# VectorE's order in the early stage of a hybrid diffusion step: activations ahead of partial sums, scan parameters later

## The chip, the cores and the metric

The kernel runs on one core of one Trainium2 chip. The metric is the time of one execution on the device in microseconds; the median of the runs is compared. The host's layout of the weights into tiles is done before and is not timed.

## What is computed

One layer of a hybrid trunk for 128 context tokens and 128 latent tokens with the same weights. The parts that matter here are those at the start:

```python
mod = silu(cond) @ w_mod + b_mod                 # (2048) @ (2048, 12288), for two conditions
sh1, sc1, g1, sh2, sc2, g2 = split(mod, 6)
xm = rmsnorm(x, norm_mix_g) * (1.0 + sc1) + sh1  # 2 x 128 tokens, 2048 channels
u, q, k, v, g_s, g_a = split(xm @ w_in)          # w_in: 2048 x 6656
```

After that come a bidirectional complex diagonal scan over `u` (64 groups of 64 states, with parameters `exp(lambda * dt)`, `B`, `C`), windowed attention over `q`, `k`, `v` with cached keys, gates, an output projection and a convolutional feed-forward block. The scan's parameters depend on the weights alone, not on the tokens.

## The kernel before, in words

**Precision.** Every large product is made of three products of fp32r halves: a weight tile `raw` is split into `hi` (ScalarE, line 184) and `lo` (VectorE, line 185), the activations into `xh`/`xl` (lines 391, 392), and TensorE adds `lo*xh`, `hi*xl`, `hi*xh` (lines 395 to 397 with weights stationary, 421 to 423 with activations stationary).

**Staging.** Columns of `xm` can be made as soon as their scale and shift columns are known. So the start of the kernel runs in seven phases over the 2048 input channels, in blocks of 128: `PHASES = (1, 1, 1, 1, 4, 4, 4)`. I count them from 0. In each phase eight groups of 512 output columns (k and v, two of q, two of u, three gates; `part_group`, line 478 on) get the products of this phase's blocks only. The result of the first phase is copied to an SBUF tile `pg`; in each later phase VectorE adds the accumulator banks to it (line 507, twice per group), and the last addition of u goes to a tile `u` (line 505). The accumulator banks are three of tag `acc` and one of tag `y`. The last phase's remaining units are taken into a later stage, woven with attention.

**Mod columns.** While a phase runs, the scale and shift columns of later phases are computed from `w_mod` (`mod_first` for one block, `mod_steps` for four; line 263): four narrow products at a time, 32 columns of the array each. Behind the last of them `mod_pp` (line 266) transposes the accumulated rows on VectorE (`macc`, line 268), adds them over the four strips with small products on TensorE (line 272) and adds the bias on VectorE into `modp` (line 276). The next phase begins with `make_xm` (line 377): scale `gsc` (line 379), the normalized transposed input `nT` scaled and shifted in place (line 390, one instruction per block and token set), the copy `xh` on ScalarE, the remainder `xl` on VectorE.

**Scan parameters.** `load_params`, `load_bc("B")`, `load_bc("C")` and `fine` of `SSM` are generators. Together they come to 22 pieces: 1 the loads of lambda, dt and states (POOL's queue); 2 to 8 some 130 small VectorE instructions on tiles `wk`, `keep`, `LB`, `LC`, `M` (128x64); 9 the loads of B (SP's queue, tile `bcn`, line 1231); 10 to 13 four blocks of copies (`cg`, ScalarE, line 1056), transpositions and copies (`bct`); 14 to 19 the same for C; 20 to 22 tables `FC` with a scratch tile `fw` (lines 1206 to 1219). `piece()` runs the next one. From phase `PIECE0` on one piece is placed behind every second unit of a phase; a phase of one block has 8 units (4 pieces), one of four blocks 16 (8 pieces). What is left is run at once behind the sixth unit of the last phase:

```python
            if p >= PIECE0 and i % PIECEN == 1:
                step(piece)
...
    step(lambda: [None for _ in gen])
```

**Order.** The program lists steps; the framework's scheduler orders each engine's queue at compile time by a simulated timeline, taking of the instructions that are ready the one with the highest priority, which is the earlier one in the program unless a block raises it. `tc.high_priority(n)` raises it by n places: splitting of weights has `HP = 300`, attention `ATTH = 300`, some later blocks `HP2 = 1000`. `tc.issue_after(ins)` keeps the instructions of the block that are on the same engine as `ins` behind it in that queue. Once ordered, each engine and each DMA queue works strictly in that order and waits where it must. Weight loads go through SP's queue in the order of the units that use them: a ring of 5 raw tiles, and 5 slots for mod weights. Tiles of 4 KB per partition (`nT`, `pg`, `nat`, `wk`, `M`, `bcn`, `bct`, `fw`, attention's `kT` and others) share a pool of 18 slots.

**Attention** starts with `att_setup` (cached keys loaded by POOL into `kT`, lines 594 and 595) and `att_k` (transposition and copy, line 604).

Of the kernel before, what the change touches and what calls it, by code (L numbers as in the profile page):

```python
# [14 lines left out]
OP = mybir.AluOpType  # L15
# [63 lines left out]
def burst(lst, pos):  # L79
    end = pos + 1  # L80
    while lst[end - 1].src is not None and lst[end - 1].frees == 0:
        end += 1
    return end


RAW, HL, W4, NS4, W2, LOADS = 5, 3, 18, 5, 3, 5
PHASES, NGA, MLEAD, PIECE0, PIECEN = (1, 1, 1, 1, 4, 4, 4), 3, 4, 2, 2
HP = 300
MRATE, AHEAD = 1.5, True
NGA2, NGS, SF0, ATT1 = 3, 4, 0.6, 1.0  # L90
# [2 lines left out]
G2A, G2B, G2S, G2C, LAG2, HP2 = 8, 8, 3, 2, 2, 1000  # L93
# [4 lines left out]
def tile_hybrid_step(ctx, tc, a):  # L98
    nc = tc.nc
    TT, TS, STT, CP = nc.vector.tensor_tensor, nc.vector.tensor_scalar, nc.vector.scalar_tensor_tensor, nc.vector.tensor_copy  # L100
# [8 lines left out]
    w4 = ctx.enter_context(tc.tile_pool(name="w4", bufs=W4))  # L109
# [12 lines left out]
    def T2(shape, name):  # L122
        return w2.tile(shape, F32, tag="w2", name=name)

    def XM(name):
        return xmp.tile([128, 4, NT], F32R, tag="xm", name=name)

    def PS(shape, tag, bufs=1):
        return ps.tile(shape, F32, tag=tag, name=tag, bufs=bufs)

    def f32(x):
        return x.bitcast(F32)
# [3 lines left out]
    def step(fn):  # L136
        steps.append(Step(fn))
# [60 lines left out]
    def wsrc(w, k0, c0, nk=2):  # L198
        v, j = w[k0 // 2, c0 // 512], k0 % 2
        return lambda raw: [(raw[:, 0:nk], v[:, j:j + nk, :])]  # L200
# [60 lines left out]
    def mod_mm(acc, kt, rhs, b, start, stop):  # L261
        j = kt % 4
        return MM(acc[32 * j:32 * j + 32], cst[:, kt, 6 - 2 * b:38 - 2 * b], rhs, start=start, stop=stop, skip_group_check=True,  # L263
           tile_position=(0, 32 * j))

    def mod_pp(acc, nb, blocks):
        m = T2([128, 512], "macc")[:, 0:acc.shape[1]]
        nc.vector.transpose(out=m, in_=acc)
        p = acc[:, 0:acc.shape[1] // 64 * nb].rearrange("p (c b s) -> p c b s", b=nb, s=2)
        mv = m.rearrange("p (c b r) -> p b c r", b=4, r=32)  # L270
        for b in range(4):
            MM(p[32 * b:32 * b + 32], i32r, mv[:, b, :, 0:2 * nb], start=True, stop=True, skip_group_check=True, tile_position=(0, 32 * b))
        for b0, c0, nc_, b, n in blocks:
            ks = slice(b0, b0 + nc_ * n)
            v = lambda t: t[:, ks].rearrange("p (b c) -> p c b", b=n)
            TT(modp[:, ks, :].rearrange("p (b c) s -> p c b s", b=n), p[:, c0:c0 + nc_, b:b + n, :],
               v(bT).unsqueeze(3).to_broadcast([128, nc_, n, 2]), OP.add)
# [18 lines left out]
    def mod_steps(gs, pool="raw"):  # L296
        nb = len(gs)
        st = {}

        def chunk(b, ku):  # L300
            def f(raw):
                if ku % 2 == 0:
                    st["r"] = raw
                    return
                if b == 0 and ku == 1:
                    st["a"] = PS([128, 512], "mod")
                prev = None
                for i, r in ((ku, raw), (ku - 1, st["r"])):
                    for j in range(2):
                        with tc.issue_after(prev.ins) if prev is not None else nullcontext():  # L310
                            prev = mod_mm(st["a"], 2 * i + j, r[:, j, :], b, b == 0 and i < 2, b + 1 == nb and i > 5)
                if b + 1 == nb and ku == 7:
                    one = all(g == gs[0] + i for i, g in enumerate(gs))
                    mod_pp(st["a"], nb, [(4 * gs[0], 0, 4, 0, nb)] if one else [(4 * g, 0, 4, i, 1) for i, g in enumerate(gs)])
            return f
        return [Step(chunk(b, ku), wsrc(a["w_mod"], 2 * ku, 512 * MOD_AT[g]), False, pool, frees=2 * (ku % 2)) for b, g in enumerate(gs) for ku in range(8)]

    def mod_first(k0, n):
        v = a["w_mod_first"]
        st = {}  # L320
        nk = 8 // n
        view = lambda raw: raw.rearrange("p a c -> p (a c)").rearrange("p (k c) -> p k c", k=nk)

        def chunk(part, ku):
            def f(raw):
                if part == 0 and ku == 0:
                    st["a"] = PS([128, 2, 128 * n], "mod")
                r = view(raw)
                for j in range(nk):
                    mod_mm(st["a"][:, part, :], nk * ku + j, r[:, j, :], 0, ku == 0 and part == 0 and j < 4, nk * ku + j >= 12)  # L330
                if part == 1 and ku == 2 * n - 1:
                    mod_pp(st["a"].rearrange("p a c -> p (a c)"), 1, [(16 + k0, 0, n, 0, 1), (k0, n, n, 0, 1)])
            return f

        def src(part, ku):
            return lambda raw: [(view(raw), v[part, k0, ku])]
        return [Step(chunk(p, ku), src(p, ku), False, "w4") for p in range(2) for ku in range(2 * n)]

    small = cpool.tile([128, 16], F32, name="small")
    nT = []  # L340
# [31 lines left out]
        nT.append(t)  # L372

    XH, XL = [], []
    gsc = cpool.tile([128, 16, 2], F32, name="gsc")

    def make_xm(k0, n):
        ks = slice(k0, k0 + n)
        STT(gsc[:, ks, :], modp[:, 16 + k0:16 + k0 + n, :], 1.0, gmix[:, ks].unsqueeze(2).to_broadcast([128, n, 2]),
            op0=OP.add, op1=OP.mult)  # L380
        m = min(n, 2)
        for k in range(k0, k0 + n, m):
            g4, o = k // 4, k % 4
            if o == 0:
                XH.append(XM("xh"))
                XL.append(XM("xl"))
            for c in range(m):
                for s in range(2):
                    v = nT[g4][:, o + c, 128 * s:128 * s + 128]
                    TS(v, v, gsc[:, k + c, s:s + 1], modp[:, k + c, s:s + 1], op0=OP.mult, op1=OP.add)  # L390
            ACT(XH[g4][:, o:o + m], nT[g4][:, o:o + m], AF.Copy)
            TT(XL[g4][:, o:o + m], nT[g4][:, o:o + m], f32(XH[g4][:, o:o + m]), OP.subtract)

    def mm3(o, wh, wl, xh, xl, start, stop):
        MM(o, wl, xh, start=start, stop=False, skip_group_check=True)  # L395
# [120 lines left out]
    def pieces(*gens):  # L516
        for g in gens:
            for _ in g:
                yield

    gen = pieces(ssm.load_params(), ssm.load_bc("B"), ssm.load_bc("C"), ssm.fine())

    def piece():
        next(gen, None)

    def sig(t):
        ACT(t, t, AF.Sigmoid)
# [27 lines left out]
    done, nw = 0, 0  # L555
    for p, n in enumerate(PHASES):
        k0 = sum(PHASES[:p])
        step(lambda k0=k0, n=n: make_xm(k0, n))
        w = [u for g in groups for u in g(k0, n)]
        if p + 1 == len(PHASES):  # L560
            steps.extend(w[:3 * n // 2])
            late = w[3 * n // 2:]
            break
        for i, x in enumerate(w):
            steps.append(x)
            nw += 1
            if xs and i % 2 == 0:
                step(xs.pop(0))
            if p >= PIECE0 and i % PIECEN == 1:
                step(piece)  # L570
            target = max(round(need[p] * (i + 1) / (len(w) - MLEAD)), round(MRATE * nw))
            while done < min(target, len(mq)) and (done < need[p] or i + 1 >= len(w) - MLEAD or AHEAD):
                end = burst(mq, done)
                steps.extend(mq[done:end])
                done = end
# [928 lines left out]
```

## Time and profile before

| | us |
|---|---|
| median of 3 runs | 1549.94 |
| lowest, highest | 1549.81, 1554.12 |
| the profiled execution's own time | 1552.15 |
| its span, first to last instruction | 1550.1 |
| mean granted TensorE clock (1 is full) | 0.99 |

All windows and starts below are microseconds from the start of this span. Engines: PE is TensorE's products, PEld its weight loads, DVE VectorE, ACT ScalarE, POOL GpSimd, SPq and POOLq the DMA queues of SyncE and GpSimd. A busy PE is a modelled figure, since products are pipelined; the starts are measured.

### The profile page before, as it was taken

The numbers are of one execution on the slowest core, as the hardware profiler recorded it, in microseconds if no ns is written. First come the engines' busy times: TensorE is split into PE (matmuls) and PEld (weight loads), VectorE is DVE, ScalarE is ACT, GpSimd is POOL, SyncE is SP. The second block draws the span as 40 slices with busy tenths as digits, with TensorE's granted clock in tenths as the row PEclk, the third lists the DMA queues.
The fourth block names the chain that finished last, engine by engine and source line by source line (L and its number), as shares of the span: only waits on it lengthen the run. The fifth ranks groups of instructions, "written<-read, shape, count | busy, mean of one in ns | idle before, by whom it ended". The sixth has DMA issues, their size and how long they took to land.

```text
span 1550.1 us, 29294 instructions
## 1 busy us (share of the span) xinstructions
PE 1491.0 (96%) x11871; PEld 1311.1 (85%) x11871; DVE 1007.7 (65%) x1541; ACT 766.7 (49%) x1191; POOL 85.7 (6%) x179
## 2 busy tenths in 40 slices
PE   6989999999899999999999999999999999999997
PEld 5758799778677788998689999889999988999986
DVE  4997776468866566765665656655665655666665
ACT  6335537645545666544554544433544543545543
POOL 2000004022321000000000000000000000000000
PEclk9999999999999999999999999999999999999999
DMA  9999754774676677975566676765555565566563
GB/s 352 352 340 321 286 196 157 258 277 156 209 241 238 240 250 274 310 244 192 172 242 235 205 245 201 238 200 190 176 192 181 181 197 191 175 205 197 170 203 123
DMA packets 104246, 349.18 MB, mean 225 GB/s; under 512 B 13900, under 2 KB 16628, under 8 KB 104112
## 3 DMA queue, kind: packets, MB, share of 16 engines
q1 hardware_dynamic: 98576, 344.20, 64.9%
q0 software_dynamic: 5312, 3.05, 0.8%
q8 instruction: 93, 1.52, 0.4%
q14 instruction: 41, 0.34, 0.1%
q10 hardware_dynamic: 224, 0.08, 0.0%
HBM read 343.76 MB, written 2.46 MB: 223 GB/s over the span
## 4 chain that ended last, share of the span: by engine, by line
PE 83%; DMA 8%; DVE 4%; ACT 2%; issue 1%; POOL 1%; SPq 0%; DVEq 0%; ACTq 0%
PE acc L395 16%; PE acc L396 16%; PE acc L397 16%; PE acc L421 8%; PE acc L422 8%; PE acc L423 8%; PE mod L263 5%; DMA raw<-in_w_mod_dram 2%; DMA raw<-in_w_in_dram 2%; PE bu L1375 1%; DVE lo L185 1%; DMA rw<-in_w_mod_dram 1%; DMA U<-u 1%; DMA raw<-in_w_attn_o_dram 1%; ACT hi L184 1%
## 5 line engine op out<-in xcount | busy, mean ns | idle before, releaser
L185 DVE TENSOR_TENSOR lo<-raw,hi 128x1024 fp32r<-128x1024 f32 (+1 forms) x456 | 538.7, 1186 | 444.8 <-ACT hi L184 442.8
L184 ACT ACTIVATE hi<-raw 128x1024 fp32r<-128x1024 f32 (+1 forms) x456 | 468.5, 1029 | 609.1 <-PE acc L397 260.7
L395 PE MATMUL acc<-yh,lo 128*128 128x256 f32 x1408 | 400.0, 284 | 0.0
L396 PE MATMUL acc<-yl,hi 128*128 128x256 f32 x1408 | 398.8, 283 | 0.0
L397 PE MATMUL acc<-yh,hi 128*128 128x256 f32 x1408 | 398.7, 283 | 0.0
L395 PEld LDWEIGHTS acc<-yh,lo 128*128 128x128 f32 x1408 | 270.3, 192 | 8.9 <-DVE lo L185 4.2
L396 PEld LDWEIGHTS acc<-yl,hi 128*128 128x128 f32 x1408 | 270.3, 192 | 0.1
L397 PEld LDWEIGHTS acc<-yh,hi 128*128 128x128 f32 x1408 | 270.2, 192 | 0.0
L395 PE MATMUL acc<-xh,lo 128*128 128x256 f32 x568 | 166.8, 294 | 9.3 <-ACT sig L672 4.8
L396 PE MATMUL acc<-xl,hi 128*128 128x256 f32 x568 | 163.4, 288 | 0.0
L397 PE MATMUL acc<-xh,hi 128*128 128x256 f32 x568 | 163.1, 287 | 0.0
L422 PE MATMUL acc<-lo,ff 128*128 128x512 f32 x352 | 136.8, 389 | 0.0
L423 PE MATMUL acc<-hi,ff 128*128 128x512 f32 x352 | 136.8, 389 | 0.0
L395 PEld LDWEIGHTS acc<-xh,lo 128*128 128x128 f32 x568 | 109.2, 192 | 31.4 <-DVE lo L185 6.9
L421 PE MATMUL acc<-hi,ff 128*128 128x512 f32 x352 | 127.8, 390 | 0.0
L396 PEld LDWEIGHTS acc<-xl,hi 128*128 128x128 f32 x568 | 109.6, 193 | 2.4 <-issue 2.2
L397 PEld LDWEIGHTS acc<-xh,hi 128*128 128x128 f32 x568 | 109.5, 193 | 0.7 <-issue 0.7
L263 PE MATMUL mod<-raw,cst 128*32 128x512 f32 x480 | 72.2, 631 | 8.0 <-DMA raw<-in_w_mod_dram 7.2
L421 PEld LDWEIGHTS acc<-hi,ff 128*128 128x128 f32 x352 | 66.1, 188 | 14.7 <-issue 1.1
L423 PEld LDWEIGHTS acc<-hi,ff 128*128 128x128 f32 x352 | 66.1, 188 | 13.7
L422 PEld LDWEIGHTS acc<-lo,ff 128*128 128x128 f32 x352 | 66.1, 188 | 13.5
L1316 POOL DMA_DIRECT2D U<-u x128 | 62.6, 497 | 159.6 <-PE bu L1375 138.5
(365 smaller groups left out, 2149.3 us busy)
## 6 DMA issues: line engine op xcount, KB each, us to landing
raw<-in_w_up_dram SPq DMA_DIRECT2D x176, 512.0 KB, 4.2
raw<-in_w_mod_dram SPq DMA_DIRECT2D x120, 512.0 KB, 5.1
raw<-in_w_in_dram SPq DMA_DIRECT2D x88, 512.0 KB, 4.5
raw<-in_w_down_dram SPq DMA_DIRECT2D x88, 512.0 KB, 4.3
rw<-in_w_mod_dram SPq DMA_DIRECT2D x56, 512.0 KB, 6.6
raw<-in_w_out_dram SPq DMA_DIRECT2D x32, 512.0 KB, 4.1
rw<-in_w_mod_first_dram SPq DMA_DIRECT2D x16, 512.0 KB, 7.4
raw<-in_w_in_dram SPq DMA_DIRECT2D x32, 256.0 KB, 6.1
```

The source lines that it names most:

```text
L184: ACT(th[:, w], raws[n][:, w], AF.Copy)
L185: TT(tl[:, w], raws[n][:, w], f32(th[:, w]), OP.subtract)
L263: return MM(acc[32 * j:32 * j + 32], cst[:, kt, 6 - 2 * b:38 - 2 * b], rhs, start=start, stop=stop, skip_group_check=True, tile_position=( ...
L395: MM(o, wl, xh, start=start, stop=False, skip_group_check=True)
L396: MM(o, wh, xl, start=False, stop=False, skip_group_check=True)
L397: MM(o, wh, xh, start=False, stop=stop, skip_group_check=True)
L421: MM(accs[s], xl, hi[:, j, :], start=(kt == first), stop=False)
L422: MM(accs[s], xh, lo[:, j, :], start=False, stop=False)
L423: lastmm[0] = MM(accs[s], xh, hi[:, j, :], start=False, stop=(kt == last - 1))
L1316: nc.gpsimd.dma_start(G["U4", qd][32 * e:32 * e + 32, q, :], u[32 * q:32 * q + 32, 64 * e:64 * e + 64])
L1375: MM(bu[:, ri, x], BL[d][:, ri, q, :], u[:, :, ::-1] if d else u, start=(x == 0), stop=True, skip_group_check=True)
```

## The change

`mod_pp` of the mod columns that the phases need and `make_xm` of every phase are placed in blocks of priority 1000. `PIECE0` goes from 2 to 4, so that the first piece stands in phase 4 instead of phase 2. The instructions of a piece that are on VectorE are ordered behind the last `xl` that `make_xm` has issued. The arithmetic is the same.

```diff
-PHASES, NGA, MLEAD, PIECE0, PIECEN = (1, 1, 1, 1, 4, 4, 4), 3, 4, 2, 2
+PHASES, NGA, MLEAD, PIECE0, PIECEN = (1, 1, 1, 1, 4, 4, 4), 3, 4, 4, 2
...
                     one = all(g == gs[0] + i for i, g in enumerate(gs))
-                    mod_pp(st["a"], nb, [(4 * gs[0], 0, 4, 0, nb)] if one else [(4 * g, 0, 4, i, 1) for i, g in enumerate(gs)])
+                    with tc.high_priority(HP2) if pool == "w4" else nullcontext():
+                        mod_pp(st["a"], nb, [(4 * gs[0], 0, 4, 0, nb)] if one else [(4 * g, 0, 4, i, 1) for i, g in enumerate(gs)])
...
                 if part == 1 and ku == 2 * n - 1:
-                    mod_pp(st["a"].rearrange("p a c -> p (a c)"), 1, [(16 + k0, 0, n, 0, 1), (k0, n, n, 0, 1)])
+                    with tc.high_priority(HP2):
+                        mod_pp(st["a"].rearrange("p a c -> p (a c)"), 1, [(16 + k0, 0, n, 0, 1), (k0, n, n, 0, 1)])
...
+    xlast = [None]
...
-            TT(XL[g4][:, o:o + m], nT[g4][:, o:o + m], f32(XH[g4][:, o:o + m]), OP.subtract)
+            xlast[0] = TT(XL[g4][:, o:o + m], nT[g4][:, o:o + m], f32(XH[g4][:, o:o + m]), OP.subtract)
+
+    def xm_first(k0, n):
+        with tc.high_priority(HP2):
+            make_xm(k0, n)
...
     def piece():
-        next(gen, None)
+        with tc.issue_after(xlast[0].ins):
+            next(gen, None)
...
-        step(lambda k0=k0, n=n: make_xm(k0, n))
+        step(lambda k0=k0, n=n: xm_first(k0, n))
```

## Rows read from the trace of the kernel before

**Rows 1.** The page, part 1: busy time, share of the span, instructions.

```profile
PE 1491.0 (96%) x11871; PEld 1311.1 (85%) x11871; DVE 1007.7 (65%) x1541; ACT 766.7 (49%) x1191; POOL 85.7 (6%) x179
```

**Rows 2.** Windows by stage: window and length, busy us by engine, clock, DMA share, GB/s.

```profile
40.00:97.00 57.00, 49.53 (x397) 35.48 (x396) 55.18 (x133) 19.07 (x31) 0.00 (x0) 0.99 0.99 361
97.00:142.00 45.00, 45.00 (x295) 34.16 (x295) 41.20 (x145) 20.09 (x43) 0.00 (x0) 0.97 0.93 308
142.00:193.00 51.00, 50.53 (x354) 40.16 (x353) 36.63 (x60) 26.51 (x69) 3.38 (x7) 1.00 0.86 301
193.00:229.00 36.00, 36.00 (x238) 32.96 (x237) 27.12 (x36) 14.32 (x16) 1.26 (x3) 1.00 0.59 197
```

**Rows 3.** TensorE in order of time: start, us, line, operation, [idle before <-releaser].

```profile
66.79 0.35 PE L395 MATMUL acc<-xh,lo 128*128 128x256 f32 x1 [0.99 <-DVE lo L185]
...
86.19 0.36 PE L395 MATMUL acc<-xh,lo 128*128 128x256 f32 x1 [0.91 <-DVE lo L185]
...
89.23 1.93 PE L263 MATMUL mod<-rw,cst 128*32 128x512 f32 x16
96.58 0.77 PE L421 MATMUL acc<-hi,xl 128*128 128x512 f32 x1 [5.43 <-DVE wk L1133]
...
100.14 0.40 PE L421 MATMUL acc<-hi,xl 128*128 128x512 f32 x1
100.38 0.39 PE L422 MATMUL acc<-lo,xh 128*128 128x512 f32 x1
```

**Rows 4.** Windows of 5 us, same columns as in rows 2.

```profile
95.00:100.00 5.00, 3.42 (x9) 2.75 (x10) 5.00 (x20) 1.07 (x2) 0.00 (x0) 0.66 1.02 409
100.00:105.00 5.00, 5.00 (x27) 3.19 (x25) 4.97 (x26) 1.68 (x2) 0.00 (x0) 1.00 0.42 163
105.00:110.00 5.00, 5.00 (x26) 3.22 (x25) 4.90 (x25) 2.08 (x2) 0.00 (x0) 1.00 0.91 330
```

**Rows 5.** VectorE in order of time, the activations of phase 4.

```profile
83.19 0.71 DVE L268 STREAM_TRANSPOSE macc<-mod 128x512 f32<-128x512 f32 x1
...
87.97 0.23 DVE L276 TENSOR_TENSOR modp<-mod,vecA 128x8 f32<-128x8 f32 x2
...
88.35 1.28 DVE L507 TENSOR_TENSOR pg<-acc,pg 128x512 f32<-128x512 f32 x2
89.54 0.16 DVE L379 SCALAR_TENSOR_TENSOR gsc<-modp,vecA 128x8 f32<-128x8 f32 x1
...
92.19 0.59 DVE L390 TENSOR_SCALAR nT<-nT,gsc,modp 128x128 f32<-128x128 f32 x2
...
95.74 0.69 DVE L392 TENSOR_TENSOR xl<-nT,xh 128x512 fp32r<-128x512 f32 x1
```

**Rows 6.** ScalarE in order of time: `xh` of phase 4, and the cached keys.

```profile
93.47 0.63 ACT L391 ACTIVATE xh<-nT 128x512 fp32r<-128x512 f32 x1 [2.75 <-DVE nT L390]
...
228.34 0.39 ACT L604 ACTIVATE kT<-misc 128x256 f32<-128x256 f32 x1 [0.59 <-PE misc L603]
```

**Rows 7.** Windows of VectorE's instructions on tile `wk` alone: busy us (count), clock, DMA.

```profile
40.00:97.00 57.00, 6.66 (x35) 0.99 0.99 361
97.00:142.00 45.00, 17.05 (x98) 0.97 0.93 308
```

**Rows 8.** DMA issues to 250 us: tensor, queue, count, KB each, median us to landing.

```profile
bcn<-in_ssm_c_re_dram SPq DMA_DIRECT2D x4, 128.0 KB, 10.5
```

**Rows 9.** The chain that ended last, in order of time: start, us, what.

```profile
124.44 8.45 DMA rw<-in_w_mod_dram
132.91 10.60 DMA bcn<-in_ssm_c_re_dram
143.57 9.35 DMA rw<-in_w_mod_dram
```

**Rows 10.** Window of VectorE's instructions on tile `FC` alone.

```profile
142.00:200.00 58.00, 7.89 (x18) 1.00 0.83 289
```

**Rows 11.** POOL in order of time: the load of the cached keys.

```profile
177.22 0.57 POOL L594 DMA_DIRECT2D kT<-in_cache_k_dram  x1 [28.35 <-DVE fw L1218]
```

## The prediction

> **What bounds the kernel now.** I began with the page's first part: TensorE is busy for 1491 of 1550.1 us [rows 1]. That is a modelled figure, so the next question is where TensorE truly stands still early, in the stage that the change touches. A table of windows, cut at the moments when TensorE starts a phase of four input blocks, gives it [rows 2]: between 40 and 97 us VectorE is busy 55.18 of 57.00 us and TensorE 49.53; in the two windows after that TensorE is full (45.00 of 45.00, 50.53 of 51.00) and VectorE is not (41.20, 36.63). So only the first of the three windows is a VectorE stage.
>
> TensorE's own order in time shows the loss [rows 3]. It ends phase 3 with a double group of mod products that starts at 89.23 and lasts 1.93 us, then is idle 5.43 us, to 96.58. Two smaller stops of 0.99 and 0.91 us, at 66.79 and 86.19, wait for a weight's `lo` half on VectorE. The idle time also costs speed: in the slice from 95 to 100 us the granted clock is 0.66 [rows 4], a mixture of the 1.2 and 2.4 GHz levels after a stop. Nine products from 96.58 to 100.14 took 3.56 us; at the spacing just after (100.14 to 100.38, 0.24 us) they take 2.1. That is 1.45 us more.
>
> What TensorE waited for stands in VectorE's order [rows 5]. The partial sums of the shift and scale columns are transposed at 83.19, their last step `modp` runs at 87.97, the scale at 89.54, the first `nT` at 92.19 and the first `xl` at 95.74, so the new activations are ready at 96.43. Alone, the chain takes transposition 0.71, TensorE group and `modp` about 0.5, scale 0.16, four `nT` at 0.27 each from start to start, ScalarE copy 0.63 [rows 6], `xl` 0.69: 3.8 us. The other 9.4 us went to the `pg` sums of phase 3, weight halves and scan parameters that VectorE put in between; one pair of `pg` sums stands there at 88.35.
>
> **The change, part by part.** *Priority of `mod_pp` and `make_xm`.* Nothing is added; about 9 us of waiting leaves the chain. The activations can be ready at 83.19 + 3.8 = 87.0, before TensorE runs out at 91.16. The 5.43 us and the 1.45 us go. What is late next are the `pg` sums that were passed: their accumulator banks come free later by the length of the chain's VectorE work, about 3 us, and weight halves yield as well. The cover is the mod groups (1.93 us for the last two).
>
> *Scan parameters two phases later, behind `xl`.* 35 instructions on the scratch tile leave the window 40 to 97, and the 98 after it become 133 [rows 7]. The 35 are 6.66 us long, but neighbours on VectorE overlap: two `pg` sums take 1.28 us together and one `xl` of the same shape 0.69 [rows 5], so 0.10 us each, and the 35 occupy 6.66 at most and 3.2 at least. I take 4.7, near the middle. This should cut the two `lo` stops; I take 1.0 of 1.9 us, bounds 0 and 1.9. The same 4.7 us land in the window 97 to 142: 41.20 + 4.7 = 45.9 in 45.0. It overflows by 0.9 us, which I charge; bounds 0 (the next window has 14 us free) and 4.7 (all given back through late banks). The wait itself holds nothing up: `xl` of the same phase is already first in the queue, and behind it only these instructions carry the edge.
>
> *DMAs that move with it.* On POOL, the few small loads of parameters come later, before a phase that needs nothing from them. On SP's queue the eight B loads leave the middle of phase 4 and go to the start of phase 5, the eight C loads from there to its end; a load is 128 KB and one of C took 10.5 us to land [rows 8]. This matters, since from 124 to 153 the chain of waits is a string of loads, 8.45, 10.60 (a C load) and 9.35 us [rows 9]: TensorE is full there, with the loads just in time. If it arrives earlier, the loads must too. Room: SP's stream was idle for 58% of 100 to 105 us and 9% of 105 to 110 [rows 4], 2.9 + 0.45 = 3.35 us, and 1.05 MB of B loads at the stage's 361 GB/s [rows 2] is another 2.9. Together 6.25 us. C goes from that place, but B takes it, so C counts nothing.
>
> *The rest.* Pieces 17 to 22 (three C blocks and the fine tables) no longer fit into phase 5 and run at once after six units of phase 6. The 18 table operations are 7.89 us [rows 10], in a window with VectorE 27.12 busy of 36.00 [rows 2]; I cost them at nothing because 8.9 us are free. If that cover is gone, see the slow rival. Transposes and ScalarE copies of B and C only move.
>
> **Sum.** 5.43 + 1.45 + 1.0 - 0.9 = 7.0 us, capped by the loads at 6.25. The profiled execution took 1552.15 us around its span of 1550.1, 2.2 above the median of 1549.94; both should drop alike, the first to 1545.9, the median to **1543.7**. Bounds of this case: without overflow or cap 5.43 + 1.45 + 1.9 = 8.8; with nothing from the `lo` stops and half of the overflow's 4.7 given back 5.43 + 1.45 - 2.35 = 4.5, at the edge of what can be told.
>
> One rule bears on how much there is to win. The Trainium skill, page "Perfetto Trace Analysis", section "Identifying the Most-Contended Engine", holds matmul busy time a bad measure and judges TensorE's headroom by the busy share of weight loads. By it, the window 40 to 97 with 35.48 of 57 us [rows 2] against 92% in 193 to 229 would have 16.8 us to give, and the sum would end near 1533.
>
> **Rivals.** (a) *More than the stop was lost.* Weight loads fill 62% of the window 40 to 97 and 92% later [rows 2]; if the difference is lost time, 0.92 x 57 - 35.48 = 16.8 us, 1533 to 1541. Against it: products of 512 columns start every 0.24 us outside the few stops [rows 3], and each takes one weight load, so their share is low without a loss. The rule of the Trainium skill quoted above is this case; the trace speaks against it. 0.08.
>
> (b) *The loads stay the bound.* B in the place of C costs as much as C did, so only the idle 3.35 us are won: 1546.6. For it: the string of loads [rows 9]. Against it: SP can run ahead in phase 4. 0.13.
>
> (c) *VectorE's work is conserved.* The stop goes from 97 into phase 4, where the parameters, older in program order, pass the `pg` sums; 4.7 us and the passed sums come back, only the clock's 1.45 us stay: 1548.5. For it: 45.9 of 45 us. 0.14.
>
> (d) *Slower: attention waits for a buffer.* POOL's load of the cached keys waited for the last table operation and went out at 177.22 [rows 11]; its keys are copied at 228.34, 51 us later [rows 6]. Phase 6 now begins near 193 - 6 = 187, its six units take 6 x 12 x 0.24 = 17 us, and 7.9 us of tables in the quarter of VectorE left free need 32: 236 against a need of 222. If the slot is the same one, TensorE stands 14 us before the scores: 1557.7. It decides once the last table operation ends after 222. Against it: four `nT` tiles of the same pool are released at phase 6's start, and nothing forces the same slot. 0.12.
>
> (e) *Nothing changes*, because the order on the queues comes out alike or other waits fill the gap: 1549.9. 0.05.
>
> **The numbers.** Forecast 0.48, the rest as above. A measurement of this kernel can tell about 0.3%, 4.65 us, from no change. Faster than 1545.3: the forecast and (a), 0.56; within: (b), (c), (e), 0.32; slower: (d), 0.12. The range takes all of the forecast, (b), (c), (e), the nearer part of (a) and the smaller delays of (d): 1538 to 1553, leaving out about 0.15.
>
> **What would show it.** Right: no TensorE idle time above 1 us between 80 and 100 us; the granted clock 1.0 there; `modp` and `nT` directly behind the transposition; phase 4's first product near 90 and phase 5's and 6's six to seven us earlier; no scratch-tile instruction before phase 4's `xl`. Wrong: a new TensorE stop in 100 to 150 that ends on a mod load or a B load (then b) or on a `pg` sum (then c); the cached keys' load issued after 215 with a stop at the scores (then d). If all of the early steps come out and the total does not, later stages gave it back.

## The result, and the profile after

The changed kernel takes 1567.32 us (median of 4 runs, 1566.83 to 1568.67), the kernel before beside it 1552.03: a ratio of 1.0101, 95% interval 1.0074 to 1.0127. It is slower by 15 us, where I forecast 6 us faster; the range missed it. The profiled execution took 1568.67 us around a span of 1566.8. Part 1 of its page, and the windows by stage, in the columns of [rows 2]:

```profile
PE 1503.9 (96%) x11871; PEld 1320.1 (84%) x11871; DVE 1009.1 (64%) x1541; ACT 762.1 (49%) x1188; POOL 85.6 (5%) x179
```

```profile
40.00:97.00 57.00, 51.66 (x419) 37.04 (x417) 52.10 (x100) 21.16 (x34) 0.00 (x0) 1.00 0.96 354
97.00:142.00 45.00, 44.58 (x300) 34.12 (x304) 37.00 (x107) 14.72 (x17) 0.00 (x0) 1.00 0.93 341
142.00:193.00 51.00, 51.00 (x355) 40.94 (x354) 43.31 (x121) 22.63 (x45) 0.00 (x0) 1.00 0.93 301
193.00:229.00 36.00, 36.00 (x239) 32.83 (x237) 28.81 (x46) 19.50 (x50) 3.09 (x5) 1.00 0.61 194
```

Nothing here is 15 us longer. Against [rows 2], TensorE gained 2.1 us in the first window, the clock is full in both of the first two, and VectorE's load has moved from the second window (41.20 to 37.00) to the third (36.63 to 43.31). The first `xl` of phase 6 starts at 189.15 us, before at 192.41. So the loss comes later, and up to phase 6 the change gains 3 us. That gain is made late: the first `xl` of phase 5 still starts at 141.26 us, before at 140.76.

What comes late is the attention. In the kernel before, the last B or C block was copied out at 191.31 us, ahead of phase 6. Now the last two B blocks (194.12 and 200.57 us) and all four C blocks (214.24 to 235.31) are copied out in phase 6, with the fine tables on VectorE. Each block is collected in the PSUM bank `misc`, which the attention's transposes use too. ScalarE and then TensorE of the changed kernel in order of time:

```profile
235.31 0.66 ACT L1253 ACTIVATE bct<-misc 128x256 f32<-128x256 f32 x2 [1.24 <-PE misc L1251]
236.49 0.38 ACT L612 ACTIVATE kT<-misc 128x256 f32<-128x256 f32 x1 [0.53 <-PE misc L611]
...
241.23 0.39 ACT L612 ACTIVATE kT<-misc 128x256 f32<-128x256 f32 x1 [0.28 <-PE misc L611]
```

```profile
234.89 0.38 PE L1251 MATMUL misc<-kc,cg 128*128 128x128 f32 x2
236.02 0.44 PE L611 MATMUL misc<-kc,pg 128*128 128x128 f32 x2 [0.75 <-ACT bct L1253]
...
247.06 1.06 PE L633 MATMUL bu<-kT,pg 128*128 128x128 f32 x8
```

The first keys are transposed in the microsecond after the last C block is copied out, at 236.02. The last keys follow at 241.23 (before at 228.34, [rows 6]), the first scores at 247.06 (before 235.60) and the first scan at 351.79 (before 336.72). The first scan before, then after:

```profile
336.72 1.22 DVE L1397 TENSOR_TENSOR_SCAN vv<-R,vv 128x512 f32<-128x512 f32 x1
```

```profile
351.79 1.21 DVE L1405 TENSOR_TENSOR_SCAN vv<-R,vv 128x512 f32<-128x512 f32 x1
```

TensorE has weight products to do meanwhile, so these 15 us of lateness are not yet lost time.

They become lost time near 400 us. The load queue stands there for a place in the ring of five weight tiles; its rows in the kernel before and in the changed one:

```profile
377.86 19.06 SPq L155 DMA_DIRECT2D raw<-in_w_mod_dram  x2
```

```profile
374.33 43.16 SPq L155 DMA_DIRECT2D raw<-in_w_mod_dram  x2
```

The view of the queue's waits names the mod products (L263): the longest wait is 18.4 us before and 42.5 after. These tiles hold modulation weights whose products need the one `mod` bank, and that bank comes free only behind VectorE's transposition of the group before (L268). The last products of that group, before and after, and then VectorE before and after:

```profile
353.00 1.93 PE L263 MATMUL mod<-raw,cst 128*32 128x512 f32 x16
```

```profile
357.86 1.07 PE L263 MATMUL mod<-raw,cst 128*32 128x512 f32 x8
```

```profile
391.48 0.70 DVE L268 STREAM_TRANSPOSE macc<-mod 128x512 f32<-128x512 f32 x1
392.11 1.18 DVE L1397 TENSOR_TENSOR_SCAN vv<-R,vv 128x512 f32<-128x512 f32 x1
```

```profile
410.44 0.68 DVE L1397 TENSOR_TENSOR t<-bu,tab 128x512 f32<-128x512 f32 x1
411.04 0.70 DVE L268 STREAM_TRANSPOSE macc<-mod 128x512 f32<-128x512 f32 x1
411.67 1.18 DVE L1405 TENSOR_TENSOR_SCAN vv<-R,vv 128x512 f32<-128x512 f32 x1
```

The group's products ended at 354.9 us before and at 358.9 after, so the transposition came 36.6 and 52.1 us after its data. In both it stands 0.63 us ahead of the fifth scan: its result `macc` comes from the same ring of three temporaries as the scan's `t` and `pr`. My reading is that this ties it to the scan in VectorE's order; mod_rows_in_own_tile below tests it. The scans came 15 to 20 us later, and the modulation group only 4. What that does to TensorE, in windows of the kernel before and of the changed one (columns as in [rows 2]):

```profile
340.00:360.00 20.00, 20.00 (x169) 17.20 (x170) 14.45 (x23) 11.53 (x24) 0.00 (x0) 1.00 0.78 280
360.00:380.00 20.00, 18.46 (x278) 17.11 (x278) 18.53 (x35) 16.71 (x38) 7.81 (x16) 1.00 0.41 138
380.00:400.00 20.00, 15.59 (x251) 11.25 (x249) 17.81 (x35) 12.03 (x35) 7.82 (x16) 0.83 0.18 58
400.00:420.00 20.00, 19.76 (x258) 15.26 (x259) 14.00 (x21) 7.26 (x13) 5.42 (x12) 1.00 0.76 254
```

```profile
340.00:360.00 20.00, 17.31 (x153) 12.57 (x154) 16.93 (x31) 8.19 (x20) 7.86 (x16) 1.00 0.64 220
360.00:380.00 20.00, 19.62 (x184) 19.02 (x187) 15.51 (x25) 8.15 (x15) 5.25 (x11) 1.00 0.54 189
380.00:400.00 20.00, 12.75 (x193) 10.74 (x181) 14.45 (x29) 14.63 (x38) 2.56 (x6) 0.65 0.02 4
400.00:420.00 20.00, 15.46 (x217) 12.07 (x216) 13.50 (x28) 9.82 (x28) 7.81 (x16) 0.58 0.12 36
```

For 40 us almost nothing is loaded (4 and 36 GB/s), TensorE has little but the scan's small products, and its granted clock falls to 0.65 and 0.58, between its levels of 1.2 and 2.4 GHz. An estimate of the work done is busy time times granted clock: before 20.00 + 18.46 + 15.59 x 0.83 + 19.76 = 71.2 us at full clock, after 17.31 + 19.62 + 12.75 x 0.65 + 15.46 x 0.58 = 54.2. The 17 us that are missing, less the 3 us by which phase 6 is ahead, are about the 15.3 us of the result.

### The profile page after: what moved, and what is told of

Its sections match the earlier page's. It is cut to its first block, busy times and chain, and to the rows that moved or that the text cites. A ratio compares the mean times of both kernels' runs of the same rounds, so it can differ in the third digit from the quotient of the medians.

```text
span 1566.8 us, 29298 instructions
## 1 busy us (share of the span) xinstructions
PE 1503.9 (96%) x11871; PEld 1320.1 (84%) x11871; DVE 1009.1 (64%) x1541; ACT 762.1 (49%) x1188; POOL 85.6 (5%) x179
## 4 chain that ended last, share of the span: by engine, by line
PE 85%; DMA 6%; ACT 4%; DVE 3%; issue 1%; POOL 1%; SPq 0%; ACTq 0%; DVEq 0%
PE acc L402 16%; PE acc L404 16%; PE acc L403 16%; PE acc L429 8%; PE acc L428 8%; PE acc L430 8%; PE mod L263 5%; DMA raw<-in_w_in_dram 2%; DMA raw<-in_w_mod_dram 2%; PE bu L1383 1%; DVE lo L185 1%; DMA raw<-in_w_attn_o_dram 1%; ACT hi L184 1%; POOL U L1324 1%; ACT CL L1337 1%
## 5 line engine op out<-in xcount | busy, mean ns | idle before, releaser
L263 PE MATMUL mod<-raw,cst 128*32 128x512 f32 x480 | 73.3, 629 | 8.0 <-DMA raw<-in_w_mod_dram 7.9
```

## The experiments

The theory I set out with: the pieces that start in phase 4 leave C blocks for phase 6, these hold the attention, the scan comes late, and the end with it. The rivals: the new priorities do the harm; or the load-queue stall has a cause of its own. The fifteen kernels differ only in order, banks and buffers.

**Which part, and which place?** Pieces back to phase 2 in the changed kernel:

```
-PIECE0 = 4
+PIECE0 = 2
```

> The changed kernel with the parameter pieces put back to start in phase 2 (early priorities and the queue edge kept). Theory 'late pieces': the C blocks and the fine tables end before the last phase again, first scores at 230 to 238 us (247.0 in the changed kernel), first scan at 330 to 340 us, end 1540 to 1553 us, ratio to the kernel before 0.993 to 1.002. Rival 'the priorities cost it': end stays at 1560 us or more. Rival 'the late load-queue stall alone': the scan comes earlier but the stall behind the mod products near 380 us is still 35 us or more, and the end stays above 1558 us.

Measured: 1551.09 us, ratio 0.9986 (0.9964 to 1.0008); first scores 236.00, first scan 339.61, longest wait of the queue 17.6 us. As 'late pieces' said; the priorities are not the harm, but with early pieces they win nothing either.

The kernel before with the pieces alone:

```
-PIECE0 = 2
+PIECE0 = 4
```

> The kernel before with nothing changed but the first phase of the pieces, 4 for 2. Theory 'late pieces': first scores at 244 to 250 us, first scan at 348 to 356 us, end 1562 to 1572 us, ratio 1.006 to 1.013. Rival 'the priorities cost it': within 3 us of the kernel before, ratio 0.998 to 1.002.

Measured: 1580.28 us, ratio 1.0172 (1.0140 to 1.0204); first scores 249.90, first scan 354.07, wait 42.6. The late pieces are the part that costs, and the size was missed: they cost 28 us, of which the other two parts of the change win 11 (by the ratios) to 13 (by the medians) back.

The late modulation sums in a tile of their own (the weight tile whose products have just run):

```
-def mod_pp(acc, nb, blocks):
-    m = T2([128, 512], "macc")[:, 0:acc.shape[1]]
+def mod_pp(acc, nb, blocks, own=None):
+    m = (T2([128, 512], "macc") if own is None else own)[:, 0:acc.shape[1]]
...
-mod_pp(st["a"], nb, ...)
+mod_pp(st["a"], nb, ..., raw[:, 1, :] if pool == "raw" else None)
```

> The changed kernel with the transposed sums of the three late modulation groups written over the weights they came from, and not into the ring of three temporaries that the scan uses; nothing of the early stage is changed. Theory 'late pieces': the first scan stays at 350 to 353 us; what the stall adds is 42.5 - 18.4 = 24 us of load-queue wait, of which the end gets back 3 to 8 us, end 1560 to 1564 us. Rival 'the late load-queue stall alone': the transposition moves from 411 us to 358 to 375 us, the longest wait of the load queue falls below 10 us and the end comes to 1545 to 1555 us, ratio 0.995 to 1.002, though the scan starts as late as before.

Measured: 1547.28 us, ratio 0.9962 (0.9942 to 0.9981). Here my theory fell and the rival's numbers came. VectorE of this kernel, then its windows:

```profile
360.75 0.72 DVE L268 STREAM_TRANSPOSE raw<-mod 128x512 f32<-128x512 f32 x1 [2.82 <-PE mod L263]
```

```profile
340.00:360.00 20.00, 17.59 (x142) 12.59 (x138) 15.84 (x29) 7.91 (x19) 7.88 (x16) 0.88 0.71 245
360.00:380.00 20.00, 20.00 (x171) 18.09 (x168) 13.73 (x22) 7.22 (x12) 2.40 (x5) 0.95 0.63 208
380.00:400.00 20.00, 19.12 (x277) 14.44 (x275) 15.13 (x28) 15.61 (x38) 5.45 (x12) 1.00 0.67 232
400.00:420.00 20.00, 18.35 (x255) 15.06 (x254) 17.54 (x26) 8.79 (x18) 7.84 (x16) 1.00 0.57 199
```

The transposition now waits for its own product (which ended at 360.68) and for nothing else; the queue's longest wait for mod products in 340 to 430 us is 6.3 us (9.9 over the whole kernel, at a later place where the kernel before has it too), the loads run on at 199 to 245 GB/s and the clock is back. The same estimate gives 17.59 x 0.88 + 20.00 x 0.95 + 19.12 + 18.35 = 72.0 us of work, 17.8 more than in the changed kernel, for 20 us of time. And the first scan is as late as ever, at 351.01. A late scan by itself costs nothing here.

The B and C blocks in the bank of the scores:

```
-p = PS([128, 4, 2, 2, 32], "misc")
+p = PS([128, 4, 2, 2, 32], "bu")
```

> The changed kernel with the B and C blocks transposed into the bank of the scores and scan inputs instead of the one that the attention's transposes use. Theory 'the bank holds the attention': the cached keys are transposed at 215 to 225 us (236.0), first scores at 234 to 241 us (247.0), end 1552 to 1562 us. Rival 'ScalarE and VectorE hold it': the C blocks still take both engines up to 233 us, first scores at 245 us or later, end 1563 to 1570 us.

Measured: 1550.13 us, ratio 0.9982 (0.9962 to 1.0003), even below the range for the bank. TensorE of this kernel:

```profile
215.69 0.39 PE L611 MATMUL misc<-kc,pg 128*128 128x128 f32 x2
218.91 0.38 PE L1251 MATMUL bu<-kc,cg 128*128 128x128 f32 x2
...
237.16 1.16 PE L633 MATMUL bu<-kT,pg 128*128 128x128 f32 x8 [0.85 <-ACT bct L1253]
```

Keys are transposed between the C blocks, 20 us earlier, though the blocks take as long as before. The first scan comes at 341.00 and the queue's wait is 18.4 again. The Trainium skill, page "Perfetto Trace Analysis", section "Optimizing Tensor Performance", asks that independent groups of matmuls rotate through different banks so that one can be emptied while the next runs. This case agrees: moving the blocks to another bank is worth 17 us, but only through a stall 160 us later.

So two unlike cures, at the two ends of one chain, each give the whole loss back: bank, late scan, stall.

**Does lateness have a price without the stall?** The own tile in the kernel before (before_own_tile), with the pieces at 2 in the changed kernel (early_pieces_own_tile), with the other bank (own_tile_other_bank), and with late pieces alone (late_pieces_own_tile).

> The kernel before with only the late modulation sums in a tile of their own. Theory 'the ring stall prices lateness': before's own stall of 18.4 us cost it, by the proportion of the changed kernel (20 us of end for 42.5 - 6.3 = 36 us of wait), (18.4 - 6.3) x 20 / 36 = 7 us: 1542 to 1549 us, ratio 0.993 to 0.998. Rival 'only a long stall costs': 1549 to 1555 us, ratio 0.998 to 1.002.

> The changed kernel with its pieces back in phase 2 and the late modulation sums in a tile of their own. Theory 'the ring stall prices lateness': within 3 us of the kernel before with its own tile, as the two were alike with the stall (ratio 0.9986), 1541 to 1549 us. Rival 'the early priorities gain when nothing later takes it': 3 to 6 us below that kernel.

> The changed kernel with both: the late modulation sums in their own tile and the B and C blocks in the other bank. Theory 'the ring stall prices lateness': the late attention costs next to nothing once the stall is gone, so this is within 3 us of the changed kernel with its own tile alone (1547 us): 1543 to 1549 us. Rival 'late attention has a price of its own' and the early gain of my forecast (6 us) shows at last: 1537 to 1542 us.

> The kernel before with the pieces from phase 4 (no priorities) and the late modulation sums in a tile of their own; with the shared ring it took 1580 us. Theory 'the ring stall prices lateness': 20 us or more come back, 1550 to 1560 us, as 8 to 12 us of the 28 were lost in the early stage without the priorities. Rival 'late attention has a price of its own': 1565 us or more. First scan at 352 to 356 us under both.

Measured, in this order: 1548.46 us, ratio 0.9963 (0.9946 to 0.9981); 1548.90, 0.9970 (0.9956 to 0.9985); 1545.86, 0.9960 (0.9939 to 0.9981); 1552.45, 0.9986 (0.9971 to 1.0001). The last had taken 1580.28 with the shared ring: the ring alone made 28 us of it. The kernel before paid 5.6 us for the ring, with its wait of 18.4. The attention's start (first scan at 340.62 or at 351.01) makes no difference that these runs can tell.

**Can the early gain come through?** Three pieces for every four units, with the shared ring (dense_pieces) and with the own tile:

```
-if p >= PIECE0 and i % PIECEN == 1:
+if p >= PIECE0 and i % 4:
```

> The changed kernel with three pieces for every four of its units in phases 4 and 5 instead of one for every two, so that all 22 end before phase 6; the ring of temporaries stays shared. Theory 'late attention meets the ring stall': cached keys transposed at 215 to 229 us, first scores at 233 to 238 us, load-queue stall 16 to 22 us, end 1547 to 1554 us (ratio 0.996 to 1.001). Rival 'any late start of the pieces costs it': first scores after 242 us, stall above 30 us, end above 1560 us.

> The same dense pieces with the late modulation sums in a tile of their own. If what the early stage gained (phase 6 starts 3 us earlier, 189 against 192 us) is lost again in phase 6 to the C blocks and fine tables, then moving these before phase 6 lets it through: 1541 to 1545 us, 2 to 5 us below the changed kernel with its own tile. Rival 'something later takes up any few us': 1546 to 1550 us, ratio 0.995 to 0.998 like the other three with this tile.

With the shared ring 1567.61 us, ratio 1.0093 (1.0065 to 1.0120): a miss for my reading. The pieces stand ahead of phase 6 in the program, but the C blocks still ran in it. ScalarE and the load queue of dense_pieces:

```profile
227.37 0.66 ACT L1253 ACTIVATE bct<-misc 128x256 f32<-128x256 f32 x2 [1.67 <-PE misc L1251]
231.21 0.37 ACT L612 ACTIVATE kT<-misc 128x256 f32<-128x256 f32 x1
```

```profile
368.17 39.62 SPq L155 DMA_DIRECT2D raw<-in_w_mod_dram  x2
```

First scores 244.13, first scan 343.43, only 2.4 us later than with the other bank; but the modulation group ended at 351.8, 8 us earlier than there, and the wait is 38.9. So the wait goes with the distance between the group and the fifth scan, not with the scan's time. With the own tile the same order is the fastest kernel of the study: 1541.86 us, ratio 0.9928 (0.9901 to 0.9956), its first scores as late as 245.35. The order of the change itself, with that tile, stayed level with the kernel before with it (0.9962 and 0.9963), so there the early 3 us did not reach the end.

The queue edge alone taken out of the changed kernel, and pieces from phase 3 with the own tile:

```
-with tc.issue_after(xlast[0].ins):
-    next(gen, None)
+next(gen, None)
```

> The changed kernel without the edge that queues the pieces' VectorE work behind the last activations; the late start and the priorities stay. Theory 'late attention meets the ring stall': first scores at 244 to 250 us, load-queue stall 38 us or more, end 1562 to 1574 us. Rival 'the edge holds the pieces back': first scores before 240 us, stall below 25 us, end 1547 to 1556 us.

> The changed kernel with its pieces from phase 3 (20 of the 22 have a place before phase 6, 16 in the change) and the late modulation sums in a tile of their own. If phase 6 gives back the early gain: 1541 to 1546 us. Rival 'something later takes up any few us': 1546 to 1550 us.

Without the edge 1578.22 us, ratio 1.0152 (1.0121 to 1.0183), above the 1574 that I had allowed: phase 6 starts at 193.77 instead of 189.15, the wait is 42.5. The edge holds nothing back; it is the part that clears the early stage. Without it 32 instructions on the scratch tile (6.07 us) run ahead of 97 us, though the pieces start in phase 4, and TensorE stops before phase 4 as long as in [rows 3]:

```profile
99.15 0.77 PE L428 MATMUL acc<-hi,xl 128*128 128x512 f32 x1 [5.29 <-DVE wk L1110]
```

This stop is 2.0 to 2.7 us in the seven kernels that have the edge and the pieces from phase 4, and 5.1 to 5.4 us in the ten others, with the priorities or without. By the estimate of busy time times clock, the kernel without the edge lacks 5.2 us of work against the changed one in 97 to 142 us (39.4 and 44.6) and 5.4 us in 340 to 440 (66.9 and 72.3, in slices of 20 us). That is about the 11 us by which it is slower.

From phase 3: 1550.18, 0.9983 (0.9965 to 1.0002), phase 6 at 195.40: an earlier place for the pieces takes the early gain away.

**Which part makes the early gain?** The dense kernel with its own tile, given the other bank, or without the priorities and the edge, or without the edge alone.

> Dense pieces, own tile for the late modulation sums, and the B and C blocks in the other bank: attention should start 6 to 10 us earlier than without the bank (first scores at 235 to 240 us instead of 245). Theory 'lateness alone is free': within 2 us of the 1541.9 us without the bank, ratio 0.990 to 0.995. Rival 'late attention has a price of its own once the stall is gone': 1534 to 1539 us, ratio below 0.990.

> The kernel before with the pieces dense in phases 4 and 5 and the late modulation sums in a tile of their own, and none of the priorities or the queue edge. If the priorities and the edge carry the early gain (phase 6 at 190 us instead of 192 to 195): 1546 to 1552 us, ratio 0.995 to 0.999. If the places of the pieces carry it: 1540 to 1544 us, ratio 0.991 to 0.995.

> Dense pieces, own tile and the priorities, without the edge that queues the pieces' VectorE work behind the last activations. If the edge is what keeps the parameters' work out of the activations' way: phase 6 at 193 us or later, 1547 to 1553 us, ratio 0.995 to 1.000. If the priorities do it alone: phase 6 at 190 us, 1540 to 1544 us.

Measured: 1544.87 us, ratio 0.9954 (0.9936 to 0.9971); 1547.76, 0.9974 (0.9961 to 0.9988); 1548.25, 0.9978 (0.9961 to 0.9994). The bank brought the first scores to 232.07, 13 us earlier, and no gain (3.0 us above the kernel without it, where I had allowed 2): lateness alone is free here. The priorities without the edge win nothing: phase 6 starts at 195.23 us, without both at 195.33, with both at 189.92 (188.93 with the other bank). Together they are worth 3 to 8 us by the ratios; only the upper figure, against the dense kernel with its own tile alone, is clear of the intervals. No run has the edge without the priorities, so what these add to it is not shown.

The chain in one table, all in us. "Gap" is from the end of the first late modulation group's last product to its transposition; the wait is the queue's longest for mod products in 340 to 430 us.

| kernel | phase 6, first `xl` | first scan | gap | longest wait | ratio |
|---|---|---|---|---|---|
| before | 192.41 | 336.72 | 36.6 | 18.4 | 1 |
| pieces_from_phase2 | 192.95 | 339.61 | 36.6 | 17.6 | 0.9986 |
| c_blocks_other_bank | 189.06 | 341.00 | 36.5 | 18.4 | 0.9982 |
| dense_pieces | 188.70 | 343.43 | 49.4 | 38.9 | 1.0093 |
| the change | 189.15 | 351.79 | 52.1 | 42.5 | 1.0101 |
| no_queue_edge | 193.77 | 354.80 | 53.2 | 42.5 | 1.0152 |
| late_pieces_alone | 192.37 | 354.07 | 53.0 | 42.6 | 1.0172 |
| late_pieces_own_tile | 191.20 | 354.45 | 0.1 | 5.2 | 0.9986 |
| mod_rows_in_own_tile | 189.28 | 351.01 | 0.1 | 6.3 | 0.9962 |
| dense_pieces_own_tile | 189.92 | 344.26 | 0.1 | 6.4 | 0.9928 |

With the shared ring the transposition stands 0.63 us ahead of the fifth scan in all seven kernels. What the runs leave open: why the modulation group falls 36.5 us ahead of that scan in some orders and 49 us or more in others; why the dense C blocks still run in phase 6; and why phase 5 is shorter in the changed kernel (47.9 us between the first `xl` of phases 5 and 6, before 51.7).

## Why the prediction was wrong

**What bounds the kernel: right for the early stage, too narrow for the end.** I read the stretch to 229 us and took what it wins as what the kernel wins. The windows of the kernel before at 380 to 400 us (58 GB/s, clock 0.83) and the 18.4 us wait of its queue were there to read; they are not in my rows.

**Priority of `mod_pp` and `make_xm`: the direction right, the size off, and the wrong part credited.** I set 5.43 + 1.45 us, from a chain of 3.8 us. TensorE and VectorE after:

```profile
84.74 0.39 PE L402 MATMUL acc<-xh,lo 128*128 128x256 f32 x1 [0.67 <-DVE lo L185]
...
97.42 0.47 PE L428 MATMUL acc<-hi,xl 128*128 128x512 f32 x1 [2.56 <-DVE xl L395]
```

```profile
87.53 0.72 DVE L268 STREAM_TRANSPOSE macc<-mod 128x512 f32<-128x512 f32 x1 [0.36 <-PE mod L263]
...
90.79 0.23 DVE L276 TENSOR_TENSOR modp<-mod,vecA 128x8 f32<-128x8 f32 x2
90.94 0.68 DVE L514 TENSOR_TENSOR pg<-acc,pg 128x512 f32<-128x512 f32 x1
91.53 0.15 DVE L382 SCALAR_TENSOR_TENSOR gsc<-modp,vecA 128x8 f32<-128x8 f32 x1
...
94.86 1.22 DVE L185 TENSOR_TENSOR lo<-raw,hi 128x1024 fp32r<-128x1024 f32 x1
95.99 0.68 DVE L514 TENSOR_TENSOR pg<-y,pg 128x512 f32<-128x512 f32 x1
96.59 0.68 DVE L395 TENSOR_TENSOR xl<-nT,xh 128x512 fp32r<-128x512 f32 x1
```

The stop is 2.56 us for 5.43, and the clock stays full (in own_tile_other_bank, behind a stop of 2.0 us, it is 0.66 at 95 to 100 us). But the first product comes at 97.42, not near 90: `pg` sums and weight halves still stand between the chain's steps, from the transposition to the end of the first `xl` it takes 9.7 us (13.2 in [rows 5], 3.8 forecast). And the transposition itself starts 4.3 us later than at 83.19: the mod products that it waits for ended at 87.44, before at 82.04, about 2.5 us of which come from slower loads (last section; phase 3's `xl` started at 57.95, before at 55.48). The step that failed is "about 9 us of waiting leaves the chain": it was 3.5. And the edge, of which I wrote "The wait itself holds nothing up" and to which I gave no gain, is needed for what did leave: with the priorities and without it the stop is 5.29 us (no_queue_edge).

**Scan parameters later: the move as forecast, its gain not.** No scratch-tile instruction runs before 97 us. But the stops for a weight's `lo` half, two with 1.9 us before, are four with 3.2 us (0.5 to 1.5 each); of the 1.0 us that I took for them nothing came. Phase 6 is 3.3 us earlier, where I forecast six to seven for it and for phase 5, and phase 5's first `xl` is 0.5 us later. So about half of the sum of 7.0 was there at phase 6, but it was made in phase 5, at another place than I said, and I can't claim it for my terms. The overflow of VectorE that I charged in phase 4 did not come (37.00 of 45 us).

**The rest: the step that decided, and that failed.** "Pieces 17 to 22 no longer fit into phase 5 and run at once ...; I cost them at nothing because 8.9 us are free." I counted VectorE's time for the tables and left the C blocks at "only move". VectorE's time was not the matter: the blocks hold a PSUM bank that the next step needs, and c_blocks_other_bank shows it to be worth all of the loss (17 us back). I listed the instructions that move, and not the bank that they hold while they wait.

**The rivals.** (d), the slower one, had the place and the sign: the attention waits for a buffer, 14 us. POOL's row after:

```profile
215.49 0.54 POOL L602 DMA_DIRECT2D kT<-in_cache_k_dram  x1
```

That is the issue after 215 which I had named as its sign. But the keys were there in 5 us and the bank was not, and TensorE did not stand before the scores; the price was paid at 374 to 417 us. That it came near 14 us is no merit of the rival. I gave it 0.12. (a), that all the time without weight loads is lost: their busy time in 40 to 97 us rose by 1.6 us only, from 35.48 to 37.04, while the stop halved. The fastest kernel of the study (1541.86 us) stops just short of its 1541, and largely by what it won at the stall (the own tile alone gives 5.6 us in the kernel before); so nothing here shows the 16.8 us as headroom. (b), (c) and (e) do not explain a loss.

**The numbers.** The range ended at 1553, below the 1557.7 of my only slow case, because I gave that 0.12 and left out its larger part; the result lies 10 us above even that. My last sentence on signs, that later stages may give it back if the early steps come out, is near to what happened, though the early steps came out only in part; it had no chance of its own among the rivals.

## What to carry to other kernels

When a step is moved, list the buffers and banks that it holds as well as the engines it uses, and who takes them next. A step that came late cost nothing here while there was other work; look for the place where its order is tied to another stream, as here by a shared ring of temporaries, for there lateness turns into a standing queue. Before changing an order that reaches so far, cut such ties: the own tile gives 0.37% in the kernel before and takes 1.4 to 1.9% off each of the three slow orders that were tried with it.

## What the runs showed of the hardware

The same early code loads at two rates. Windows of own_tile_other_bank, then of mod_rows_in_own_tile, whose first phases have the same edit:

```profile
20.00:40.00 20.00, 19.64 (x244) 16.49 (x245) 11.31 (x28) 15.21 (x30) 3.07 (x7) 1.00 1.02 372
```

```profile
20.00:40.00 20.00, 19.53 (x229) 16.00 (x225) 9.48 (x24) 13.55 (x27) 3.23 (x7) 1.00 0.94 347
```

At 372 GB/s the second phase's `xl` starts at 32.93 us, at 347 GB/s at 34.80, and the 1.9 us stay up to phase 4 (first `xl` at 94.84 and 96.70); at phase 6 only 0.5 us of it is left (188.77 and 189.28). Of the 16 profiled kernels beside the one before, seven were of the slower kind (340 to 348 GB/s in this window), the changed kernel among them (34.66), with the edit or without it; the nine others had 366 to 378 GB/s, the kernel before 385 (32.19). So about 2 us of any comparison up to phase 4 here belong to neither edit.

In 400 to 420 us the changed kernel, which had run little but small scan products since 380 us, was granted 0.58 of TensorE's clock; the kernel with the own tile, whose weight products ran on, had 1.00 in the same window. The standing load queue thus costs twice: the weight products that are missing, and the lower clock on the work that is left.
